# Moving the sums of six activation mixes from VectorE to GpSimd in the down projections

## The chip, the cores and the metric

The kernel runs on one core of a Trainium2 chip. The metric is the device time in microseconds of one execution; the time before is the median of three runs.

## What is computed

The reference is a two-layer streaming encoder on 512 positions of width 1024, in float32. Each layer has a token mixer and a gated ConvFFN, each behind an RMSNorm and with a residual. The part that the change touches is the end of the ConvFFN, the product with `w_down`:

```python
def conv_ffn(h, w_up, conv_w, conv_b, w_down):
    u, v = jnp.split(h @ w_up, 2, axis=-1)
    u = causal_dwconv(u, conv_w, conv_b)
    return (jax.nn.gelu(u, approximate=False) * v) @ w_down

for l in range(DEPTH):
    ...
    x = x + y                      # y: token mixer of layer l
    x = x + conv_ffn(rmsnorm(x, ffn_norm[l]), ffn_w_up[l], ffn_conv_w[l], ffn_conv_b[l], ffn_w_down[l])
return rmsnorm(x, final_norm)
```

The inner width is 2816, that is 22 tiles of 128 channels by 512 positions.

## The kernel before

Activations lie with channels on the 128 partitions and the 512 positions along the free dimension. Every float32 product is made from three products of rounded parts: a value is split into `hi` (a rounding copy on ScalarE) and `lo = value - hi` (on VectorE), and TensorE computes hi x hi, hi x lo and lo x hi. Weights are split in the same way, block by block, a few microseconds before their use.

Large products use a Strassen-like scheme with seven block products in place of eight (`seven_product`), named p1 to p7. It needs sums of weight blocks, and mixes (sums and differences) of activation halves: the left and right 256 positions, and two channel tiles that form a pair.

In a down stage (one per layer) the 22 inner tiles are used in two ways. The first 10 (`NPLAIN`) go into plain products (`down`, names `mh` and `ml`). The other 12 form six pairs, `DOWN_LEFT[i]` and `DOWN_RIGHT[i]`, that feed four seven-products (`down_seven`). The plain products of output tiles 0 to 5 run first, 180 matmuls; while they run, `mix_m` (L773) prepares the six pairs, one about every 5.7 us by the plan (`MIXT`). The steps of one mix are:

- `low_part` and `right_part`: splits (hi on ScalarE, lo on VectorE; tiles `bh` and `bl`) of the left tile's first half and of the whole right tile, the operands of p1, p2 and p3.
- `sums` (L787 to L792): four instructions on 128x256 halves that overwrite the two tiles (`cacc` in the profile), each but the first reading the one before. The first two finish the left tile, the last two the right one.
- `ta_part` and `tb_part`: splits of the two mixed tiles (`xh`, `xl` for the first four pairs, `eh`, `el` for the other two), the operands of p5 and p7, and of p6 and p4. The seven-products run in the order p1, p2, p6, p5, p7, p3, p4.

The order of the work on TensorE, VectorE and ScalarE is written out by hand: each step is entered with `at(time, step)`, the steps are sorted by time, and each of these three engines issues its instructions in that order. A time is thus a place in the order and not a promise. GpSimd and SyncE are not among the planned engines, and the scheduler of the language orders what they issue:

```python
planned = (mybir.EngineType.PE, mybir.EngineType.DVE, mybir.EngineType.Activation)
```

Beside the sums, a down stage issues accumulating DMAs from GpSimd's queue: `add_sum` (L477) for the weights of each of the four seven-products (tile `s`, from `in_w_ds`), and one for the extra columns of the first (`queued_sum`, L557, tile `raw_e`, from `in_w_de`). `extra_weights` makes the last two of the six pairs' weights, with the parts `hi_e` and `lo_e`.

Of the kernel before, what the change touches and what calls it, by code (L numbers as in the profile page):

```python
# [12 lines left out]
ALU = mybir.AluOpType  # L13
# [69 lines left out]
def trunk_kernel(ctx, tc, xT, cols, w_first, w_lead, w_ab, w_pool, w_abo, w_vg, w_qk, w_r, w_g2, w_go, w_up, w_dn, w_ds, w_de, out):  # L83
    nc = tc.nc
    V, S, G, PE = nc.vector, nc.scalar, nc.gpsimd, nc.tensor
# [9 lines left out]
    def slot(dt=F32, name="s"):  # L95
        return big.tile([P, T], dt, tag="s", name=name)
# [89 lines left out]
    def split(hi, lo, src):  # L186
        S.activation(hi, src, AF.Copy)  # L187
        V.tensor_tensor(lo, src, f32(hi), ALU.subtract)
# [195 lines left out]
    lo_t, hi_t = slice(0, H), slice(H, T)  # L384
# [56 lines left out]
    def at(t, fn):  # L441
        events.append((t, len(events), fn))
# [246 lines left out]
    def ffn(l, acc, mixed, finish, ahead, halves_last=False):  # L689
# [83 lines left out]
        def mix_m(i, t):  # L773
            def low_part():
                if i % 2 == 0:
                    mixed_m["b1", i // 2] = slot(F32R, "bh"), slot(F32R, "bl")
                h, lo = [b[:, i % 2 * H : i % 2 * H + H] for b in mixed_m["b1", i // 2]]
                mixed_m["p1", i] = h, lo
                split(h, lo, ms[DOWN_LEFT[i]][:, lo_t])

            def right_part():
                h, lo = slot(F32R, "bh"), slot(F32R, "bl")
                split(h, lo, ms[DOWN_RIGHT[i]])
                mixed_m["p2", i] = h[:, lo_t], lo[:, lo_t]
                mixed_m["p3", i] = h[:, hi_t], lo[:, hi_t]

            def sums():  # L787
                m1, m2 = ms[DOWN_LEFT[i]], ms[DOWN_RIGHT[i]]
                V.tensor_tensor(m1[:, lo_t], m1[:, lo_t], m1[:, hi_t], ALU.subtract)
                V.tensor_tensor(m1[:, hi_t], m2[:, hi_t], m1[:, hi_t], ALU.subtract)  # L790
                V.tensor_tensor(m2[:, hi_t], m1[:, lo_t], m2[:, hi_t], ALU.add)
                V.tensor_tensor(m2[:, lo_t], m2[:, hi_t], m2[:, lo_t], ALU.subtract)  # L792

            def ta_part():
                h, lo = (xh[i], xl[i]) if i < HK else (slot(F32R, "eh"), slot(F32R, "el"))
                split(h, lo, ms[DOWN_LEFT[i]])
                mixed_m["p5", i] = h[:, lo_t], lo[:, lo_t]
                mixed_m["p7", i] = h[:, hi_t], lo[:, hi_t]

            def tb_part():  # L800
                h, lo = (xh[HK + i], xl[HK + i]) if i < HK else (slot(F32R, "eh"), slot(F32R, "el"))
                split(h, lo, ms[DOWN_RIGHT[i]])
                mixed_m["p6", i] = h[:, hi_t], lo[:, hi_t]
                mixed_m["p4", i] = h[:, lo_t], lo[:, lo_t]

            at(t, low_part)
            at(t + 0.4, right_part)
            at(t + 1.1, sums)
            at(t + 3.4, ta_part)
            at(t + 4.0, tb_part)  # L810

        for t, part in zip((5.9, 6.3, 7.99 * UNIT, 11.5, 12.0, 12.7, 13.4, 14.1), norm):
            at(t, part)
# [15 lines left out]
        for i in range(HD):  # L829
            mix_m(i, base + MIXT[i])  # L830
# [80 lines left out]
        t = base + 9 * UNIT  # L911
# [465 lines left out]
    t = 0.0  # L1377
# [353 lines left out]
```

## Time and profile before

| quantity | value |
|---|---|
| median of three runs | 997.42 us (996.09 to 997.89) |
| profiled execution | 995.26 us, span 993.6 us |
| granted TensorE clock | 0.997 |
| layer-0 plain products of the down stage | 349.71 to 390.53 us |
| layer-0 first seven-product begins | 390.54 us |
| layer-1 plain products of the down stage | 870.41 to 911.23 us |
| instructions of L789 to L792 | 12 of each line, 0.42 to 0.43 us each |

In the rows below, PE is TensorE, PEld its weight loads, DVE VectorE, ACT ScalarE, POOL GpSimd. A row of a timeline has the start in us, the duration in us, the engine, the line, the operation, output and inputs, the number of instructions merged into the row, and in brackets the idle time before it with what ended it. A row of windows has the stretch, its length, and the busy time of each engine with the number of its instructions, then the granted clock, the share of DMA and the GB/s. A row of a line's instructions gives the shortest, the median and the longest duration in ns. A row of waits has the total in us, the number of times and the longest one.

### The profile page before, as it was taken

The numbers are of one execution on the slowest core, as the hardware profiler recorded it, in microseconds if no ns is written. First come the engines' busy times: TensorE is split into PE (matmuls) and PEld (weight loads), VectorE is DVE, ScalarE is ACT, GpSimd is POOL, SyncE is SP. The second block draws the span as 40 slices with busy tenths as digits, with TensorE's granted clock in tenths as the row PEclk, the third lists the DMA queues.
The fourth block names the chain that finished last, engine by engine and source line by source line (L and its number), as shares of the span: only waits on it lengthen the run. The fifth ranks groups of instructions, "written<-read, shape, count | busy, mean of one in ns | idle before, by whom it ended". The sixth has DMA issues, their size and how long they took to land.

```text
span 993.6 us, 18580 instructions
## 1 busy us (share of the span) xinstructions
PE 984.8 (99%) x7324; PEld 932.3 (94%) x7324; DVE 881.1 (89%) x1368; ACT 621.5 (63%) x1035; POOL 88.8 (9%) x111
## 2 busy tenths in 40 slices
PE   9999999999999999999999999999999999999997
PEld 7888889999999988999999999899999999988997
DVE  7886689999999999889889789889999999899886
ACT  6432467766766666545776576667676666666553
POOL 0000111111101000002000000110110101000000
PEclk9999999999999999999999999999999999999998
DMA  7423757787787464627336453767788787454622
GB/s 252 139 91 106 175 132 177 199 196 204 202 198 184 112 156 122 173 80 185 115 103 154 107 121 113 198 152 181 200 201 203 194 209 180 117 146 125 165 81 99
DMA packets 69241, 155.22 MB, mean 156 GB/s; under 512 B 5825, under 2 KB 9281, under 8 KB 69153
## 3 DMA queue, kind: packets, MB, share of 16 engines
q1 hardware_dynamic: 50560, 119.03, 37.7%
q0 software_dynamic: 18304, 34.61, 21.1%
q8 instruction: 57, 0.93, 0.4%
q10 hardware_dynamic: 288, 0.40, 0.1%
q14 instruction: 32, 0.25, 0.1%
HBM read 149.29 MB, written 2.10 MB: 152 GB/s over the span
## 4 chain that ended last, share of the span: by engine, by line
PE 95%; DVE 2%; DMA 1%; ACT 1%; issue 0%; DVEq 0%; ACTq 0%
PE stx L611 33%; PE styz L611 19%; PE dn L274 11%; PE go L274 4%; PE abo L274 4%; PE dn L611 3%; PE stz L611 3%; PE pu L1001 2%; PE pc L274 2%; PE pb L274 2%; PE px L274 2%; PE vg L1209 2%; PE vg L1210 2%; PE vg L1211 1%; DMA raw<-in_w_up 1%; PE o L1300 1%
## 5 line engine op out<-in xcount | busy, mean ns | idle before, releaser
L501 DVE TENSOR_TENSOR lo<-raw,hi 128x1024 fp32r<-128x1024 f32 x120 | 146.3, 1220 | 9.0 <-ACT hi L495 8.6
L495 ACT ACTIVATE hi<-raw 128x1024 fp32r<-128x1024 f32 x120 | 125.5, 1058 | 38.0 <-DMA raw<-in_w_up 13.6
L477 POOL DMA_DIRECT2D s<-in_w_up x44 | 53.3, 1211 | 477.6 <-ACT yh L187 95.8
L229 ACT ACTIVATE hi<-raw 128x1024 fp32r<-128x1024 f32 (+3 forms) x69 | 61.2, 890 | 26.3 <-PE px L274 9.1
L233 DVE TENSOR_TENSOR lo<-raw,hi 128x1024 fp32r<-128x1024 f32 (+3 forms) x69 | 70.1, 1021 | 5.2 <-ACT hi L229 4.4
L370 DVE SCALAR_TENSOR_TENSOR cacc<-u,colt,cacc 128x511 f32<-128x511 f32 x96 | 71.5, 744 | 2.6 <-ACT cacc L367 2.5
L501 DVE TENSOR_TENSOR lo<-s,hi 128x1024 fp32r<-128x1024 f32 x60 | 73.1, 1218 | 0.0
L367 ACT ACTIVATE cacc<-u,colt 128x512 f32<-128x512 f32 x48 | 39.2, 817 | 44.2 <-DVE u L733 40.6
L495 ACT ACTIVATE hi<-s 128x1024 fp32r<-128x1024 f32 x60 | 63.3, 1055 | 3.5 <-issue 2.8
L611 PE MATMUL stx<-th,hi 128*128 128x256 f32 x416 | 64.6, 277 | 0.1
L611 PE MATMUL stx<-tl,hi 128*128 128x256 f32 x416 | 64.1, 276 | 0.0
L611 PE MATMUL stx<-th,lo 128*128 128x256 f32 x416 | 64.1, 276 | 0.0
L611 PE MATMUL styz<-xh,hi 128*128 128x256 f32 x400 | 62.0, 277 | 0.0
L611 PE MATMUL styz<-xh,lo 128*128 128x256 f32 x400 | 61.7, 276 | 0.0
L611 PE MATMUL styz<-xl,hi 128*128 128x256 f32 x400 | 61.6, 276 | 0.0
L611 PEld LDWEIGHTS stx<-th,hi 128*128 128x128 f32 x416 | 54.9, 188 | 0.7 <-ACT kk L718 0.2
L611 PEld LDWEIGHTS stx<-tl,hi 128*128 128x128 f32 x416 | 54.9, 188 | 0.0
L611 PEld LDWEIGHTS stx<-th,lo 128*128 128x128 f32 x416 | 54.9, 188 | 0.0
L611 PEld LDWEIGHTS styz<-xh,hi 128*128 128x128 f32 x400 | 52.9, 188 | 0.0
L611 PEld LDWEIGHTS styz<-xh,lo 128*128 128x128 f32 x400 | 52.8, 188 | 0.0
L611 PEld LDWEIGHTS styz<-xl,hi 128*128 128x128 f32 x400 | 52.8, 188 | 0.0
L495 ACT ACTIVATE sh<-raw 128x512 fp32r<-128x512 f32 x60 | 37.9, 632 | 20.7 <-DVE raw L506 20.7
(391 smaller groups left out, 2670.0 us busy)
## 6 DMA issues: line engine op xcount, KB each, us to landing
s<-in_w_up SPq DMA_DIRECT2D x44, 512.0 KB, 6.7
s<-in_w_up POOLq DMA_DIRECT2D x44, 512.0 KB, 7.0
raw<-in_w_up SPq DMA_DIRECT2D x44, 512.0 KB, 6.6
raw<-in_w_up SPq DMA_DIRECT2D x44, 256.0 KB, 3.2
raw<-in_w_dn SPq DMA_DIRECT2D x32, 320.0 KB, 2.9
raw<-in_w_ab SPq DMA_DIRECT2D x12, 512.0 KB, 3.6
raw<-in_w_abo SPq DMA_DIRECT2D x8, 512.0 KB, 3.5
s<-in_w_ds SPq DMA_DIRECT2D x8, 512.0 KB, 5.6
```

Source lines behind the costliest of these rows:

```text
L229: S.activation(parts[0], raw, AF.Copy)
L233: V.tensor_tensor(parts[1], raw, f32(parts[0]), ALU.subtract)
L274: PE.matmul(out, w[:, k, :], a[k], start=first and i == 0 and k == 0, stop=last and i == 2 and k == n - 1, skip_group_check=loose,)
L367: S.activation(acc[0], u, AF.Identity, bias=col(bname, j), scale=col(wname, 2 * nj + j))
L370: V.scalar_tensor_tensor(a, u[:, : T - i], col(wname, (2 - i) * nj + j), a, ALU.mult, ALU.add)
L477: G.dma_start(w["s31"].rearrange("p (a n) -> p a n", a=2), part, accum_op=ALU.add)
L495: S.activation(h, src(), AF.Copy)
L501: V.tensor_tensor(lo, src(), f32(h), ALU.subtract)
L611: PE.matmul(b[out][:, ts], wt[k], a[k], start=first and i == 0 and k == 0, stop=i == 2 and k == len(a) - 1, skip_group_check=True,)
L1001: PE.matmul(pus[g], parts[k][w][:, g * P : (g + 1) * P], a[k], start=k == 0 and i == 0, stop=k == KD - 1 and i == 2,)
L1209: PE.matmul(o[c][:, :n], xh[kk][:, cs], h[:, k, :], start=kk == 0, stop=False)
L1210: PE.matmul(o[c][:, :n], xl[kk][:, cs], h[:, k, :], start=False, stop=False)
```

## The change

The four instructions of `sums` are issued on GpSimd instead of VectorE, for each of the six mixes of both down stages: 48 instructions of 128x256. The splits of their results, `ta_part` and `tb_part`, are entered 1.2 us later in the plan, still ahead of the next mix's first step, which stands 5.7 us after this one's.

```diff
             def sums():
                 m1, m2 = ms[DOWN_LEFT[i]], ms[DOWN_RIGHT[i]]
-                V.tensor_tensor(m1[:, lo_t], m1[:, lo_t], m1[:, hi_t], ALU.subtract)
-                V.tensor_tensor(m1[:, hi_t], m2[:, hi_t], m1[:, hi_t], ALU.subtract)
-                V.tensor_tensor(m2[:, hi_t], m1[:, lo_t], m2[:, hi_t], ALU.add)
-                V.tensor_tensor(m2[:, lo_t], m2[:, hi_t], m2[:, lo_t], ALU.subtract)
+                G.tensor_tensor(m1[:, lo_t], m1[:, lo_t], m1[:, hi_t], ALU.subtract)
+                G.tensor_tensor(m1[:, hi_t], m2[:, hi_t], m1[:, hi_t], ALU.subtract)
+                G.tensor_tensor(m2[:, hi_t], m1[:, lo_t], m2[:, hi_t], ALU.add)
+                G.tensor_tensor(m2[:, lo_t], m2[:, hi_t], m2[:, lo_t], ALU.subtract)
...
             at(t, low_part)
             at(t + 0.4, right_part)
             at(t + 1.1, sums)
-            at(t + 3.4, ta_part)
-            at(t + 4.0, tb_part)
+            at(t + 4.6, ta_part)
+            at(t + 5.2, tb_part)
```

## The prediction

> **What bounds the kernel now.** I read the page's busy shares and chain first, then the list of what TensorE waited for, then windows of 10 us over both down stages.
>
> ```profile
> PE 984.8 (99%) x7324; PEld 932.3 (94%) x7324; DVE 881.1 (89%) x1368; ACT 621.5 (63%) x1035; POOL 88.8 (9%) x111
> PE 95%; DVE 2%; DMA 1%; ACT 1%; issue 0%; DVEq 0%; ACTq 0%
> ```
>
> ```profile
> PE warm L170 <- DVE half L176: 1.1, 1, 1.1
> PE pu L1001 <- ACT xh L995: 0.3, 1, 0.3
> PE vg L1209 <- DVE z L1157: 0.2, 1, 0.2
> ```
>
> TensorE is busy 984.8 of 993.6 us, and the waits that the profile names for it add up to 1.6 us, none of them in a down stage. The busy shares of the stretch in which the six mixes are made, first for the layer-0 stage and then for layer 1:
>
> ```profile
> core 0: us, PE busy (x) PEld busy (x) DVE busy (x) ACT busy (x) POOL busy (x), PEclk, DMA share, GB/s
> 360.00:370.00 10.00, 10.00 (x46) 8.28 (x45) 9.79 (x20) 5.59 (x11) 0.00 (x0) 1.00 0.34 97
> 370.00:380.00 10.00, 10.00 (x46) 8.29 (x45) 9.70 (x20) 6.60 (x13) 0.00 (x0) 1.00 0.34 97
> 380.00:390.00 10.00, 10.00 (x46) 8.28 (x45) 9.70 (x19) 6.15 (x11) 1.20 (x1) 1.00 0.66 159
> 390.00:396.00 6.00, 6.00 (x53) 5.92 (x52) 5.93 (x11) 3.42 (x6) 0.00 (x0) 1.00 0.26 84
> 881.00:891.00 10.00, 10.00 (x46) 8.29 (x45) 9.79 (x20) 5.91 (x12) 0.00 (x0) 1.00 0.31 85
> 891.00:901.00 10.00, 10.00 (x46) 8.29 (x45) 9.70 (x19) 6.59 (x13) 0.00 (x0) 1.00 0.32 97
> 901.00:911.00 10.00, 10.00 (x46) 8.28 (x45) 9.70 (x20) 6.14 (x11) 1.20 (x1) 1.00 0.61 153
> ```
>
> Two readings matter. TensorE has no idle time here and its granted clock is 1.00, so an earlier result on another engine cannot shorten these stages. And VectorE is nearly as full: from 360 to 396 it idles 0.21 + 0.30 + 0.30 + 0.07 = 0.88 us. It keeps pace with TensorE, but barely, so what the change does to VectorE decides. GpSimd is almost empty.
>
> **What leaves VectorE.** Consecutive rows of VectorE: the four sums of the fifth mix and what follows, with the first sum of the first and of the sixth mix.
>
> ```profile
> 360.51 0.42 DVE L789 TENSOR_TENSOR cacc<-cacc 128x256 f32<-128x256 f32 x1
> ...
> 382.62 0.42 DVE L789 TENSOR_TENSOR cacc<-cacc 128x256 f32<-128x256 f32 x1
> 383.07 0.42 DVE L790 TENSOR_TENSOR cacc<-cacc 128x256 f32<-128x256 f32 x1
> 383.52 0.42 DVE L791 TENSOR_TENSOR cacc<-cacc 128x256 f32<-128x256 f32 x1
> 383.98 0.42 DVE L792 TENSOR_TENSOR cacc<-cacc 128x256 f32<-128x256 f32 x1
> 384.33 1.47 DVE L188 TENSOR_TENSOR el<-cacc,eh 128x512 fp32r<-128x512 f32 x2
> ...
> 387.26 0.42 DVE L789 TENSOR_TENSOR cacc<-cacc 128x256 f32<-128x256 f32 x1
> ```
>
> Starts count, not spans, since spans overlap: 384.33 - 382.62 = 1.71 us for four sums. Six mixes take 6 x 1.71 = 10.3 us of VectorE in each layer. If nothing else happened VectorE would gain 10.3 us of room per layer, and the time would not move, since TensorE waits for none of it.
>
> **What GpSimd pays, and what that costs VectorE.** The profile has no GpSimd sum of two tensors. The nearest rows are its two instructions that read and write a tensor, the masks:
>
> ```profile
> 1.80 0.29 POOL L179 TENSOR_SCALAR_AFFINE_SELECT ident<-ident 128x128 f32<-128x128 f32 x1
> ...
> 467.99 1.29 POOL L1112 TENSOR_SCALAR_AFFINE_SELECT maskf<-maskf 128x512 f32<-128x512 f32 x1
> 469.22 0.52 POOL L1116 MEMSET att<- 128x512 f32 x1
> ```
>
> 128 columns take 0.29 us and 512 columns 1.29, so one column costs (1.29 - 0.29) / 384 = 2.6 ns, and 256 columns 0.29 + 128 x 0.0026 = 0.62 us. That is the value I take for a sum. It reads two operands of 256 columns; counted by what is read it would be like the 512-column row, 1.29 us, which is the upper end. I stay near the lower end because a sum writes, and steps through, 256 columns.
>
> The second mask shows more. VectorE worked at the same time, on a two-operand instruction whose other eleven occurrences are even:
>
> ```profile
> L399 DVE TENSOR_TENSOR ta<-xg x12: 415/419/855, 105.0 to 658.9; 128x256 f32<-128x256 f32 x12
> ```
>
> ```profile
> 468.69 0.85 DVE L399 TENSOR_TENSOR ta<-xg 128x256 f32<-128x256 f32 x1
> 469.58 0.48 DVE L406 SCALAR_TENSOR_TENSOR tb<-xall,colt,ta 128x256 f32<-128x256 f32 x1
> ```
>
> It took 0.85 us instead of 0.42, and its end (469.54) lies 0.26 us behind the mask's end (467.99 + 1.29 = 469.28). So it seems to have got what it needed 0.42 - 0.26 = 0.16 us before the mask's end, and to have stood still until then: it did not run more slowly, it waited. A GpSimd instruction that reads a tensor thus seems to keep such a VectorE instruction out for its span less some 0.16 us. That gives 0.62 - 0.16 = 0.46 us per sum as the lower bound, and the full 0.62 where four dependent sums stand back to back.
>
> The Trainium skill says the same more strictly (SBUF — State Buffer, section "Who interferes with whom"): a VectorE instruction with two SBUF inputs and a GpSimd instruction that reads SBUF exclude each other, and whoever comes second blocks fully until the first has ended. The one row agrees in kind (0.43 us lost in 0.59 us of overlap), and by the rule a sum would cost its whole span.
>
> Nearly all rows of VectorE in these stretches are of that kind: splits of the form lo = value - hi, and sums. So the balance of one layer, with H the time that a sum keeps VectorE out, is 24 x H that comes in, less 10.3 us that leave, less the 0.88 us that VectorE idled, less the lead that its last result had over TensorE. That lead is read at the first seven-product that takes mixed operands:
>
> ```profile
> 395.17 0.42 DVE L586 TENSOR_TENSOR lo_e<-xe,hi_e 128x256 fp32r<-128x256 f32 x1
> ```
>
> ```profile
> 395.60 0.39 PE L611 MATMUL stx<-el,hi_e 128*128 128x256 f32 x2
> 395.83 0.62 PE L611 MATMUL stx<-xh,sl 128*128 128x256 f32 x4
> 396.28 0.39 PE L611 MATMUL stx<-eh,lo_e 128*128 128x256 f32 x2
> ```
>
> VectorE finishes lo_e at 395.59 and TensorE multiplies by it at 396.28; less the load of the weights ahead of it that is a lead of about 0.6 us. Per layer 24 H - 10.3 - 0.9 - 0.6 = 24 H - 11.8. With H = 0.62 that is 14.9 - 11.8 = 3.1 us of stall, 6.2 us in the two layers. At H = 0.46 it is below zero, so nothing shows. The balance turns at H = 0.49.
>
> **The longer chain inside a mix.** ScalarE takes both splits in program order, and behind a split that waits for GpSimd stand the high parts of the next weight blocks and of the next mix. On VectorE a mix's sums took 1.71 us. On GpSimd they take 4 x 0.62 = 2.5 us, and up to two VectorE instructions of 0.7 us may come in between: 3.9 us. The later place of the two splits (1.2 us) allows for part of this. The mixes followed each other at (387.26 - 360.51) / 5 = 5.35 us. The new cycle is 3.9 us plus about 1.5 us for the high part of the second split, the first high part of the next mix and its low part: 5.4 us. That is no slower than before, so I add nothing for it; at H = 0.85 it would be 0.9 us more per mix.
>
> **GpSimd's queue.** The sums are not alone there:
>
> ```profile
> 350.08 1.20 POOL L477 DMA_DIRECT2D s<-in_w_ds  x1 [30.21 <-ACT hi L229]
> 351.88 1.20 POOL L477 DMA_DIRECT2D s<-in_w_ds  x1 [0.60 <-DMA s<-in_w_ds]
> 383.75 1.20 POOL L557 DMA_DIRECT2D raw_e<-in_w_de  x1 [30.68 <-DVE cacc L790]
> 401.20 1.21 POOL L477 DMA_DIRECT2D s<-in_w_ds  x1 [16.24 <-DMA s<-in_w_ds]
> ```
>
> Accumulating DMAs share it, and GpSimd's order is not written by the plan, so where the sums fall between them cannot be read here. Two of them are issued before the first sum (360.51), and those from 401.20 on after the sixth mix. Only the third, for raw_e, lies among the sums. Ahead of the fifth mix's sums it holds them to 383.75 + 1.20 = 384.95, 2.3 us later than 382.62; their split ended at 385.80 and TensorE used it at 395.60, so this hides. Behind all sums it is a rival, below. The two splits that move in the plan are one ScalarE and one VectorE instruction each; no DMA and no SyncE instruction moves with them.
>
> **The sum.** The profiled execution took 995.26 us, its span 993.6. Against it: 995.3 + 6.2 = 1001.5 us. This execution lies 2.2 us under the median of the runs (997.42), so for a median I say 997.4 + 6.2 = 1003.6 us. A measurement of this kernel can tell about 0.2%, 2 us, from no change; in the balance, 48 H - 23.6 for two layers, that is H = 0.53.
>
> **Rivals.**
> 1. *No slower: the sums fit into VectorE's own gaps.* If a sum keeps VectorE out for less than 0.53 us, the lost room is what VectorE no longer spends, and the lead swallows the rest. For it: the 0.46 us bound, and that GpSimd and VectorE might interleave between instructions. Against it: two operands are read where the mask read one. 997.4 us, from 995.5 to 999.4. It decides at H = 0.49.
> 2. *The sum is dearer.* With H a third of the way from 0.62 to 1.29, 0.85 us: 48 x 0.85 - 23.6 = 17.2 us, 1014.6 us. For it: reading goes twice through each column. The Trainium skill (GPSIMD Engine Reference, section 3.1) gives 4497 ns against VectorE's 2293 ns for a sum of 2048 columns; the estimate from that ratio, 0.42 x 1.96 = 0.82 us, would make it about 15.8 us. No run here shows it.
> 3. *The raw_e transfer stands behind all sums.* Its issue then moves from 383.75 to about 390.0 (387.26 + 4 x 0.62 and some waiting), and it lands 4.6 us later, at 394.6:
>
> ```profile
> DMA to landing us min/median/max: 4.4/4.6/4.8
> ```
>
> ```profile
> 393.24 0.42 DVE L571 SCALAR_TENSOR_TENSOR xe<-raw_e 128x256 f32<-128x256 f32 x1
> ```
>
> Its first reader ran at 393.24, so 1.4 us late, on top of the 3.1: 4.5 us per layer, 997.4 + 9.0 = 1006.4 us.
> 4. *Faster.* VectorE's relief would have to end a wait of TensorE. There is none in these stages, and none in the list outside them that a sum feeds. Worth 0 us at most, and so nearly excluded.
>
> **How the numbers follow.** Forecast, H between 0.53 and 0.72: 0.46, 999.4 to 1008.5 us, likeliest 1003.6. Rival 3: 0.12. Rival 2: 0.12, of which half above 1014. Rival 1: 0.25. Faster by over 0.2%: 0.05. So slower 0.46 + 0.12 + 0.12 = 0.70, same 0.25, faster 0.05. The range from 996.6 to 1014 leaves out the dearest sums (about 0.07), the faster case and the lower edge of rival 1 (about 0.10).
>
> **What would show it.** Right: GpSimd rows of 128x256 with starts about 0.6 us apart; VectorE splits of 128x512 and 128x640 beside them whose mean grows from 0.68 and 0.82 us; VectorE still full from 360 to 396; TensorE waiting some 3 us per layer at the start of the first seven-product, on a split of lo_e, el or bl. Wrong: VectorE rows of unchanged length beside GpSimd's sums, or TensorE without a gap in these windows (rival 1); starts of the sums 0.85 us apart and TensorE waiting already for the lo of the weight blocks (rival 2); VectorE or ScalarE waiting for raw_e's DMA (rival 3).

## The result and the profile after

The change makes the kernel slower: a median of 1007.79 us (1007.44 to 1008.41, four runs) against 996.75 us (995.13 to 997.89, four runs). The measured ratio is 1.0116, with a 95% interval of 1.0101 to 1.0131; that of the two medians is 1.0111. The profiled execution took 1007.44 us with a span of 1005.7 us, 12.1 us more span than before. The forecast was 1003.6 us, between 996.6 and 1014: the direction and the range held, but the sum gave 6.2 us for the 11 to 12 that came, and, as the runs show, it was not made of the right terms.

What TensorE waited for after the change:

```profile
PE stx L611 <- ACT hi L495: 5.5, 2, 3.0
PE stx L611 <- ACT hi_e L581: 1.4, 2, 0.7
PE warm L170 <- DVE half L176: 1.1, 1, 1.1
PE stx L611 <- DVE lo L501: 1.0, 1, 1.0
```

The waits of 5.5 and 1.4 us come twice, once per layer, at the first seven-product; before there was none there. The windows of layer 0, where VectorE was 97 to 98% busy before:

```profile
360.00:370.00 10.00, 10.00 (x46) 8.29 (x45) 8.54 (x11) 4.73 (x8) 6.99 (x8) 1.00 0.37 115
370.00:380.00 10.00, 10.00 (x46) 8.28 (x45) 6.98 (x9) 5.44 (x10) 6.08 (x7) 1.00 0.26 74
380.00:390.00 10.00, 10.00 (x46) 8.29 (x45) 6.39 (x9) 3.36 (x6) 6.65 (x7) 1.00 0.54 144
390.00:396.00 6.00, 3.00 (x14) 2.54 (x13) 4.72 (x6) 4.17 (x8) 3.96 (x5) 0.80 0.15 25
```

VectorE is not full any more: 8.5, 7.0 and 6.4 of 10 us. ScalarE is busy less than before, 3.4 us of the third stretch against 6.2. Neither engine is short of time, and TensorE still stands for half of 390 to 396. That is the picture of a chain, not of a full engine. GpSimd shows its links, from the third mix on:

```profile
372.39 1.12 POOL L789 TENSOR_TENSOR cacc<-cacc 128x256 f32<-128x256 f32 x1 [1.80 <-DVE bl L188]
373.58 1.20 POOL L790 TENSOR_TENSOR cacc<-cacc 128x256 f32<-128x256 f32 x1
374.86 1.20 POOL L791 TENSOR_TENSOR cacc<-cacc 128x256 f32<-128x256 f32 x1
376.14 1.07 POOL L792 TENSOR_TENSOR cacc<-cacc 128x256 f32<-128x256 f32 x1
379.01 0.74 POOL L789 TENSOR_TENSOR cacc<-cacc 128x256 f32<-128x256 f32 x1 [1.80 <-DVE bl L188]
...
386.49 1.21 POOL L557 DMA_DIRECT2D raw_e<-in_w_de  x1 [3.04 <-DMA raw<-in_w_ds]
387.27 1.20 POOL L789 TENSOR_TENSOR cacc<-cacc 128x256 f32<-128x256 f32 x1
388.55 0.74 POOL L790 TENSOR_TENSOR cacc<-cacc 128x256 f32<-128x256 f32 x1
389.37 0.74 POOL L791 TENSOR_TENSOR cacc<-cacc 128x256 f32<-128x256 f32 x1
390.19 1.07 POOL L792 TENSOR_TENSOR cacc<-cacc 128x256 f32<-128x256 f32 x1
393.06 1.11 POOL L789 TENSOR_TENSOR cacc<-cacc 128x256 f32<-128x256 f32 x1 [1.80 <-DVE bl L188]
```

An undisturbed sum takes 0.74 us and the next one starts 0.82 us after it (388.55 to 389.37). Beside VectorE's splits it takes 1.06 to 1.20 us (once 1.60, in the sixth mix), with starts 1.2 to 1.3 us apart. Four sums of the third mix last from 372.39 to 377.21, 4.8 us, where VectorE took 1.71. They form a chain because one engine runs them in order, not because each reads the one before: the second overwrites what the first has read, and the third is the first to read a result. Then GpSimd idles 1.80 us, until the next mix's split (`bl`) releases it: ScalarE must first take this mix's second split. The sums of successive mixes start 6.6 us apart here, and (393.06 - 359.36) / 5 = 6.74 us apart from the first mix (359.36) to the sixth, against 5.35 before. The `raw_e` transfer, which holds up the fifth mix, has a share in this average; without it (a run below) it is (391.37 - 359.27) / 5 = 6.42 us.

Where the lateness reaches TensorE is seen on ScalarE, before and after:

```profile
384.44 0.63 ACT L187 ACTIVATE eh<-cacc 128x512 fp32r<-128x512 f32 x1 [0.28 <-DVE cacc L792]
384.98 0.93 ACT L187 ACTIVATE bh<-cacc 128x256 fp32r<-128x256 f32 x2
385.81 1.04 ACT L495 ACTIVATE hi<-raw 128x1024 fp32r<-128x1024 f32 x1
```

```profile
389.32 0.63 ACT L187 ACTIVATE eh<-cacc 128x512 fp32r<-128x512 f32 x1 [4.37 <-POOL cacc L790]
391.29 0.63 ACT L187 ACTIVATE eh<-cacc 128x512 fp32r<-128x512 f32 x1 [1.34 <-POOL cacc L792]
391.83 0.92 ACT L187 ACTIVATE bh<-cacc 128x256 fp32r<-128x256 f32 x2
392.65 1.04 ACT L495 ACTIVATE hi<-raw 128x1024 fp32r<-128x1024 f32 x1
```

The fifth mix's second split (`eh`) runs 391.29 - 384.44 = 6.85 us later, and with it everything behind it in ScalarE's queue, among it the high part of the first seven-product's weights (L495), 6.84 us later, which has nothing to do with the mix. That part used to be done at 386.85. TensorE now asked for it at 390.74, so 3.9 us of the 6.84 were covered; the other 3.0 us are TensorE's longest wait. The rest of a layer's 6 us follows at once:

```profile
393.74 1.22 PE L611 MATMUL stx<-bh,hi 128*128 128x256 f32 x4 [3.00 <-ACT hi L495]
...
396.47 0.98 PE L611 MATMUL stx<-bh,lo 128*128 128x256 f32 x4
397.59 0.50 PE L611 MATMUL stx<-bh,lo_e 128*128 128x256 f32 x2
397.93 0.63 PE L611 MATMUL dn<-bh,hi 128*128 128x256 f32 x4
```

The product p1 takes 393.74 to 397.93, 4.2 us instead of 2.05 (390.38 to 392.43 before). Its last third needs the lo of the same weights, which VectorE delivers late (394.64 plus 1.75, and lo_e at 396.31 plus 1.22, both stretched by the sixth mix's sums). That is another 2.1 us, and about 1 us more goes at p6, of which 0.7 us is a wait for hi_e.

### The profile page after: what moved, and what is told of

Same layout as the page of the kernel before. It is cut to its first block, busy times and chain, and to the rows that moved or that the text cites. A ratio compares the mean times of both kernels' runs of the same rounds, so it can differ in the third digit from the quotient of the medians.

```text
span 1005.7 us, 18604 instructions
## 1 busy us (share of the span) xinstructions
PE 988.3 (98%) x7324; PEld 934.2 (93%) x7324; DVE 878.5 (87%) x1320; ACT 622.4 (62%) x1035; POOL 139.2 (14%) x159
## 4 chain that ended last, share of the span: by engine, by line
PE 87%; DVE 5%; POOL 4%; ACT 1%; issue 1%; DMA 1%; DVEq 0%; POOLq 0%; ACTq 0%
PE stx L611 34%; PE styz L611 20%; PE go L274 4%; PE abo L274 4%; PE dn L274 3%; PE stz L611 3%; PE dn L611 2%; PE pu L1001 2%; PE pc L274 2%; PE pb L274 2%; PE px L274 2%; PE vg L1209 2%; PE vg L1210 1%; PE vg L1211 1%; POOL cacc L792 1%
## 5 line engine op out<-in xcount | busy, mean ns | idle before, releaser
L495 ACT ACTIVATE hi<-raw 128x1024 fp32r<-128x1024 f32 x120 | 125.4, 1057 | 33.1 <-PE styz L611 11.4
L233 DVE TENSOR_TENSOR lo<-raw,hi 128x1024 fp32r<-128x1024 f32 (+3 forms) x69 | 75.7, 1104 | 5.1 <-ACT hi L229 4.4
L495 ACT ACTIVATE hi<-s 128x1024 fp32r<-128x1024 f32 x60 | 63.4, 1056 | 2.4 <-ACT sh L495 1.6
L495 ACT ACTIVATE sh<-raw 128x512 fp32r<-128x512 f32 x60 | 37.9, 632 | 21.3 <-DVE raw L506 21.3
```

The lines of the kernel that those rows point to most:

```text
L233: V.tensor_tensor(parts[1], raw, f32(parts[0]), ALU.subtract)
L495: S.activation(h, src(), AF.Copy)
```

## The experiments

Two theories stood at the start. **P**: GpSimd's sums and VectorE's splits keep each other out, which costs VectorE time and makes the chain of sums longer. **C**: the chain through GpSimd and its handovers cost by themselves. Beside them **D**, the later place of the splits, and **Q**, the raw_e transfer in GpSimd's queue. Ratios are to the kernel before, with 95% intervals, from three rounds each.

**Only the later place.** The sums stay on VectorE.

```diff
-            at(t + 3.4, ta_part)
-            at(t + 4.0, tb_part)
+            at(t + 4.6, ta_part)
+            at(t + 5.2, tb_part)
```

> Sums stay on VectorE; only the two splits are entered 1.2 us later in the plan. Theory P (the sums and VectorE's two-operand instructions keep each other out, and the longer chain of sums holds up ScalarE's splits): 0 to +1 us over the kernel before, since nothing runs on GpSimd. Rival D (the later place of the splits costs part of the loss): +3 to +6 us.

995.95 us, ratio 1.0002 (0.9993 to 1.0012). The place alone shows no cost.

**Only the other engine.** Sums on GpSimd, splits at t + 3.4 and t + 4.0 as before.

> Sums on GpSimd, the two splits at their old place. Theory P: the splits then stand ahead of a weight block's high part in some mixes, and ScalarE waits with more behind it: +10 to +14 us over the kernel before, about as the change or 1 to 3 us worse. Rival D: +5 to +8 us, better than the change by the cost of the place.

1010.04 us, ratio 1.0150 (1.0135 to 1.0165), above the change's own interval. The later place is a help of 2 to 3 us and no cost: D falls.

**raw_e without GpSimd**, in the changed kernel and, as a control, in the kernel before.

```diff
-            extra = extra_weights(w_de[l, p], base, p == 0)
+            extra = extra_weights(w_de[l, p], base, False)
```

> The change, but the weight sum raw_e is made by two VectorE instructions of 128x256 in place of the accumulating DMA in GpSimd's queue. Rival Q (the DMA's wait for its load holds up the fifth mix): the 2 us by which the fifth mix's sums are held per layer come back, +6 to +8 us over the kernel before instead of +11. Theory P without Q: +10 to +13 us, as VectorE has 0.85 us more to do per layer.

> The control for the run above: the kernel before with the same edit of raw_e. All theories: 0 to +2 us over the kernel before, from two more VectorE instructions (0.85 us) per layer in the stretch where it is full and its lead is 0.6 us.

1007.67 us, ratio 1.0125 (1.0109 to 1.0140) in the changed kernel; 996.08 us, ratio 1.0008 (0.9998 to 1.0017) in the control. The fifth mix did start earlier (385.17 for 387.27), and the wait for the weights' high part halved, but another one grew:

```profile
PE stx L611 <- ACT hi_e L581: 3.1, 2, 1.5
PE stx L611 <- ACT hi L495: 2.8, 2, 1.4
PE stx L611 <- DVE lo L501: 2.0, 2, 1.0
```

The 5.5 us of that wait became 2.8, and the 1.4 us of hi_e became 3.1, since the two new VectorE sums stand ahead of what hi_e reads. The transfer holds up GpSimd, but to take it away gains nothing by this route. How much of the loss it carries where it stands is not separated by this run.

**Sums that nobody waits for.** The kernel before, with idle sums added on GpSimd behind VectorE's own.

```diff
                 V.tensor_tensor(m2[:, lo_t], m2[:, hi_t], m2[:, lo_t], ALU.subtract)
+                idle = stage["dn"].tile([P, H], F32, tag="idle", name="idle", bufs=1)
+                for a in (m1, m1, m2, m2):
+                    G.tensor_tensor(idle, a[:, lo_t], a[:, hi_t], ALU.add)
```

> The kernel before, its sums on VectorE, and behind each mix's sums four more sums of 128x256 on GpSimd whose result nobody reads (the halves of the two tiles, added into a spare tile). No chain passes through GpSimd. Theory P, its port part: each GpSimd sum takes about 0.5 us from a VectorE that is 97% busy, 24 x 0.5 less the 1.5 us of idle time and lead is 10.5 us per layer, +15 to +25 us. Rival C (only the handover and the length of the chain cost time, the engines do not disturb each other): 0 to +1 us, VectorE's rows unchanged at 0.42, 0.68 and 0.82 us.

1018.00 us, ratio 1.0231 (1.0214 to 1.0248), 22.8 us more. The two engines disturb each other without any chain between them, which C denied. VectorE's groups from 360 to 392 in this run:

```profile
L233 DVE TENSOR_TENSOR lo<-raw,hi 128x640 fp32r<-128x640 f32 x8 | 9.1, 1151 | 0.0
L188 DVE TENSOR_TENSOR xl<-cacc,xh 128x512 fp32r<-128x512 f32 x8 | 8.4, 1088 | 0.0
L188 DVE TENSOR_TENSOR bl<-cacc,bh 128x512 fp32r<-128x512 f32 x5 | 3.4, 680 | 0.0
```

In the kernel before, the same window had 818 and 685 ns for the first two groups. The third, which runs before a mix's sums, keeps its 680 ns. What one sum costs is read from a single row of this run, an instruction that took 0.69 us in the kernel before:

```profile
363.90 1.22 DVE L760 TENSOR_TENSOR cacc<-kk,cacc 128x512 f32<-128x512 f32 x1
```

One sum beside it costs it about 0.54 us. The 128x640 split ahead of it loses as much (1.36 us instead of 0.82). The prediction's balance can be tried here: with nothing taken off VectorE it is 2 x (24 x 0.54 - 0.9 - 0.6) = 22.9 us, and 22.8 came.

**The chain without reading.** Each sum is replaced by fills of a half tile; GpSimd only writes, and reads nothing.

```diff
-                G.tensor_tensor(m1[:, lo_t], m1[:, lo_t], m1[:, hi_t], ALU.subtract)
-                ...
+                for a in (m1[:, lo_t], m1[:, hi_t], m2[:, hi_t], m2[:, lo_t]):
+                    for _ in range(3):
+                        G.memset(a, 0.5)
```

> The change, but each sum on GpSimd is replaced by three fills of the same half tile: the sums are left out, the chain through GpSimd and its handovers stay, and GpSimd reads nothing. Twelve fills at about 0.25 us give a chain of 3.0 us per mix, the length of four undisturbed sums (0.74 us each). Theory P: VectorE's rows go back to 0.68 and 0.82 us, the cycle of a mix falls under 5.35 us, 0 to +3 us over the kernel before. Rival C: the chain through GpSimd still costs, +7 to +11 us.

995.56 us, ratio 1.0002 (0.9992 to 1.0011). Nothing is lost. But the chain came out shorter than planned: three of the twelve fills do not depend on the mix's first splits and ran ahead, and the nine others took 2.6 to 3.1 us. So the run shows that handovers through GpSimd alone cost nothing, and not yet whether reading or length made the loss. The next two runs were built for that: all fills behind the first splits, twelve and sixteen of them.

```diff
-                for a in (m1[:, lo_t], m1[:, hi_t], m2[:, hi_t], m2[:, lo_t]):
+                for a in (m1[:, lo_t], m1[:, lo_t], m2[:, hi_t], m2[:, lo_t]):
-                    for _ in range(3):
+                    for _ in range(4):       # 3 in the run with twelve
```

> As the run with fills, but no fill can run ahead of the mix's first splits: twelve fills per mix (six on the left tile's first half, three on each half of the right tile), at 0.29 us each 3.5 us, about the length of four sums of 0.82 us that nothing disturbs. The sums are left out. The cycle of a mix is the chain plus the 1.7 to 1.8 us that the other run showed between chains: 5.3 us. If a mix's cycle decides: -1 to +2 us over the kernel before. If GpSimd in the chain costs by itself: +5 us or more.

> The same with sixteen fills per mix, 4.65 us, about the length of the change's disturbed sums (4.3 to 4.9 us), again without reading. The sums are left out. If the length of the cycle decides (4.65 + 1.75 = 6.4 us against the 6.2 to 6.8 us of the change): +6 to +11 us over the kernel before, with VectorE's rows at their old 0.68 and 0.82 us. If VectorE's lost time at the port decides: 0 to +2 us.

Twelve fills: 996.75 us, ratio 1.0005 (0.9988 to 1.0022). Sixteen: 1008.41 us, ratio 1.0124 (1.0107 to 1.0141), 12.9 us more and so a little above what was expected. GpSimd in the run with twelve:

```profile
366.62 3.33 POOL L791 MEMSET cacc<- 128x256 f32 x12 [2.52 <-DVE bl L188]
372.25 3.55 POOL L791 MEMSET cacc<- 128x256 f32 x12 [2.31 <-DVE bl L188]
```

The run with sixteen: GpSimd, VectorE's groups from 360 to 392, and TensorE's longest wait:

```profile
366.81 4.34 POOL L791 MEMSET cacc<- 128x256 f32 x16 [2.52 <-DVE bl L188]
373.46 4.57 POOL L791 MEMSET cacc<- 128x256 f32 x16 [2.31 <-DVE bl L188]
379.82 4.80 POOL L791 MEMSET cacc<- 128x256 f32 x16 [1.78 <-DVE bl L188]
```

```profile
L233 DVE TENSOR_TENSOR lo<-raw,hi 128x640 fp32r<-128x640 f32 x8 | 6.4, 819 | 0.0
L188 DVE TENSOR_TENSOR xl<-cacc,xh 128x512 fp32r<-128x512 f32 x8 | 5.5, 693 | 10.5 <-ACT xh L187 10.5
```

```profile
PE stx L611 <- ACT hi L495: 7.5, 2, 3.8
```

VectorE's rows are undisturbed, at 819 and 693 ns, and it idles 10.5 us for ScalarE's splits; yet the loss is that of the change, and TensorE waits for the same high part of the weights. What decides is the length of GpSimd's link, and between 3.5 us (no loss) and 4.7 us (all of it) lies the limit. An undisturbed chain of four sums, 4 x 0.82 = 3.3 us, is under the length that cost nothing here. So it seems to be the stretching of the sums by VectorE that takes the chain over the limit; no run had four undisturbed sums in the chain to show this directly.

**The splits behind the next mix's first ones**, so that GpSimd goes on while the last mix is split.

```diff
-            at(t + 4.6, ta_part)
-            at(t + 5.2, tb_part)
+            late = 2.4 if i < HD - 1 else 0.0
+            at(t + 4.6 + late, ta_part)
+            at(t + 5.2 + late, tb_part)
```

> The change with the two splits of mixes 1 to 5 entered another 2.4 us later, behind the next mix's first splits, so that GpSimd can go on to the next mix while ScalarE and VectorE split the last one. Theory P, its chain part (GpSimd, ScalarE and VectorE take turns within a mix and the cycle of 6.2 to 6.8 us is what is late): the cycle falls to GpSimd's own 4.5 to 5 us, and the loss shrinks to +1 to +5 us. If instead VectorE's lost share of the port alone decides, the loss stays at +9 to +13 us.

> The run above with the weight sum raw_e on VectorE in place of the DMA in GpSimd's queue. Rival Q: up to 4 us less than the run above. If the overlap has already taken the lateness away: the same within 1 us.

998.82 us, ratio 1.0039 (1.0024 to 1.0054); with raw_e off GpSimd 999.76 us, ratio 1.0045 (1.0030 to 1.0060), no difference between the two. A later place of two steps takes back two thirds of the loss. GpSimd and the windows in the first of these runs:

```profile
371.33 1.12 POOL L789 TENSOR_TENSOR cacc<-cacc 128x256 f32<-128x256 f32 x1 [0.36 <-DVE bl L188]
...
377.12 1.12 POOL L789 TENSOR_TENSOR cacc<-cacc 128x256 f32<-128x256 f32 x1 [1.09 <-DVE bl L188]
```

```profile
370.00:380.00 10.00, 10.00 (x46) 8.29 (x45) 10.00 (x12) 4.98 (x9) 8.15 (x8) 1.00 0.34 98
380.00:390.00 10.00, 10.00 (x46) 8.29 (x45) 10.00 (x12) 6.04 (x12) 7.31 (x8) 1.00 0.62 159
```

GpSimd idles 0.4 to 1.1 us before the second to the fourth mix instead of 1.8 to 2.5. The cycle fell to (389.32 - 360.88) / 5 = 5.7 us, not to the 4.5 to 5 us expected. Now VectorE is busy 10.0 of 10 us although the sums, 10.3 us of its work, were moved away. What remains, 3.7 us, is seen on TensorE at p1:

```profile
393.94 0.73 PE L611 MATMUL stx<-bh,lo 128*128 128x256 f32 x4 [0.31 <-DVE lo L501]
395.08 0.50 PE L611 MATMUL stx<-bh,lo_e 128*128 128x256 f32 x2 [0.40 <-DVE lo_e L586]
```

In layer 0 p1 takes 392.09 to 395.42, 3.3 us instead of 2.05, and p6 is 0.6 us longer, for a `hi_e` that waits for VectorE's `xe`. That is 1.9 us in a layer and 3.7 in both, behind a VectorE that is full. No version beat the kernel before: TensorE has no gap there that a shorter VectorE could close.

## Why the prediction was right, and where not

Direction and range held, but that the time fell so near is in part luck: the term that made most of it had been put at zero. Of the signs named, VectorE's splits did grow (128x640 from 818 to 1180 ns on average, the `xl` splits from 685 to 880), and TensorE did wait some 3 us per layer at the start of the first seven-product. But it waited for ScalarE's high part of the weights and not for a split of VectorE, VectorE was not full, and the sums' starts were 0.8 to 1.3 us apart instead of 0.6.

**TensorE has nothing to gain here.** Right: relief of VectorE brought no microsecond in any run, and rival 4 did not occur.

**The two engines keep each other out.** Right in kind, shown by the idle sums against the fills. The size H was put at 0.62 us and measures 0.54 for a full overlap. The sum itself is dearer than the masks' rows gave: 0.74 us alone, and 1.06 to 1.20 us beside VectorE. The rows were also misread. The mask of 1.29 us had itself been held up by VectorE; the same instruction in the first run with fills (L1111 there) shows it, with 740 ns:

```profile
L1111 POOL TENSOR_SCALAR_AFFINE_SELECT maskf<-maskf 128x512 f32<-128x512 f32 x1 | 0.7, 740 | 0.0
```

There the two VectorE splits of 128x544 beside it took 2.48 us together, where they took 1.90 beside the mask of 1.29: each time one side pays some 0.6 us. With 0.74 us the same reckoning by columns gives 0.29 + 128 x 0.0012 = 0.44 us for a sum, so 0.62 was nearer to the truth by luck. The undisturbed pitch of 0.82 us is the estimate that the Trainium skill's ratio gave (GPSIMD Engine Reference, section 3.1), so its rule was nearer than my rows; rival 2, at about that value, was still wrong, since it let VectorE lose the whole 0.85 us. The full blocking that the prediction took from the Trainium skill (SBUF — State Buffer, "Who interferes with whom") agrees nearly by sum: 0.74 + 0.68 = 1.42 us of the two alone, against starts 1.2 to 1.3 us apart together, so 0.1 to 0.2 us overlap and both sides pay a part. That page calls the shared port pair an exclusive lock; its words on full blocking for the whole instruction stand there with VectorE's 2-port modes.

**The balance 24 H - 11.8.** As a formula it held where it applied: 22.9 us for the idle sums, which cost 22.8. With H = 0.54 it gives 1.2 us per layer for the change, 2.3 in all, and the run with overlapped splits, where VectorE was full, lost 3.7. For the change itself it was not the term that decided: VectorE was 64 to 85% busy from 360 to 390. Rival 1, no slower below H = 0.49, was thus near as to H and wrong for another reason, the chain.

**The longer chain inside a mix: the step that failed.** I put the chain at 3.9 us, the cycle at 5.4, and added nothing. Measured are 4.0 to 5.1 us, and 6.74 us for the cycle. I had let two VectorE instructions come between the four sums of a mix; two to four of the sums are stretched, and each is longer to begin with. The runs show its price: of the 11 us, about 7 vanish when the splits are entered later, and sixteen fills without any disturbance bring all of it. At 1.4 us per cycle, five cycles long, against a cover of 3.9 us on ScalarE, the chain was the larger term.

**The lead.** I read it on VectorE, 0.6 us at lo_e. What ran out first was ScalarE's, 3.9 us at the weights' high part, behind a split that waited for GpSimd. The prediction named this queue and gave it no price.

**GpSimd's queue.** The DMA stands ahead of the fifth mix's sums, not behind all of them, so rival 3 did not occur; that its wait hides was wrong as seen on the trace (in layer 0 it starts the fifth mix's sums at 387.27, where they start at 385.17 without it), though taking it away won nothing.

## What to carry to other kernels

Work that moves to a slower engine inside a chain that three engines pass in turn lengthens the cycle of that chain, whatever it frees; add up one cycle, link by link, with durations under contention, and compare it with the pace of its consumer before counting busy time. Price a wait by all that stands behind it in the waiting engine's queue: here it was an unrelated weight block. And if the chain must pass through the slower engine, enter the waiting steps behind the next round's first steps.

## What the runs showed of the hardware

GpSimd's fills do not disturb VectorE's splits (819 and 693 ns beside them, 818 and 685 without), while each of its sums, which read, adds about 0.54 us to the VectorE instruction beside it (0.69 to 1.22 us for 128x512).

And after TensorE had stood for 3.0 us its matmuls came back slow: four of 128x256 took 1.22 us at 393.74, where the same four take 0.62 us, and the granted clock is 0.80 in the window 390 to 396 and 0.50 from 394 to 396. In the run with the splits at their old place it was so after 2.6 us (1.22 us, and a clock of 0.50 from 394 to 396), and in its layer 1 the clock was 0.50 from 924 on, some 2 us behind the end of a wait of 2.7 us. After the wait of 2.5 us in layer 1 of the change they took 0.73 us and the clock stayed at 1.00. These 0.73 us are no sign of the clock, since the four also take that after a wait of 0.3 us (393.94 above). The Trainium skill describes the halving (TensorE: Matmul & The Clock Gate, "Part 1"): the clock halves after some 3.4 us of idleness. Here waits of 2.6 to 3.0 us were enough. In the change the slow products were hidden behind the lo parts that p1 waited for.
